# Output parts 1 to 3 of both feed-forwards by seven block products, with weight sums by adding transfers and a recorded issue order

## The chip, the cores and the metric

The kernel runs on one core of one Trainium2 chip. The metric is the device time of one execution in microseconds (us), the median of the runs that are shown. A difference of about 0.3% (3 us) is what a measurement of this kernel can tell from no change.

## What is computed

One decoder block on 512 tokens of width 1024: a feed-forward, a token-mixing layer (pooling, dilated attention and gates) and a second feed-forward, each behind an RMS norm that is shifted and scaled by a condition, then a last norm. The change is in the two feed-forwards, whose hidden width `D_FF` is 2816:

```python
def swiglu(u, w_in, w_out):
    a, b = jnp.split(u @ w_in, 2, axis=-1)
    return (jax.nn.silu(a) * b) @ w_out
...
    u = modulate(rmsnorm(h, g_norm_ffn1[l]), sh1, sc1)
    h = h + 0.5 * gt1 * swiglu(u, w_ffn1_in[l], w_ffn1_out[l])
    u = modulate(rmsnorm(h, g_norm_mix[l]), sh2, sc2)
    h = h + gt2 * token_mixing(u, cos, sin, w_in[l], w_pool[l], ...)
    u = modulate(rmsnorm(h, g_norm_ffn2[l]), sh3, sc3)
    h = h + 0.5 * gt3 * swiglu(u, w_ffn2_in[l], w_ffn2_out[l])
return rmsnorm(h, g_final)
```

The vectors shift, scale and gate come from `silu(c) @ w_ada + b_ada`, 72 columns of 128 rows.

## The kernel before

**Number format.** Activations and weights are f32. Each operand of a large product is split into a high part, rounded to fp32r (`whi`, `UH`, `HI`, `SH`), and the rest (`wlo`, `UL`, `HK`, `SL`), and a product is three matmuls: high by high, high by low, low by high (`mm3`, L364; inside `product`, L751 to L753). Everything is transposed: 128 features on the partitions, 512 tokens along the free axis.

**Weights.** A *chunk* is 128x1024 f32, 512 KB. The queue of SyncE (SP) loads it into one of a few buffers (`raw`, `X`). ScalarE (ACT) writes its high part into the ring `whi` (`split_hi`, L319) and VectorE (DVE) the rest into `wlo` (`split_lo`, L336). The rings hold seven chunks. `look(4)` puts the splits four chunks ahead of the matmuls. In the second feed-forward, the chunks of output parts 0 to 3 (`self.added`) have the rest made differently: ACT writes the negative high part into `wlo`, and GpSimd (POOL) issues a transfer that adds the raw chunk to it (L334).

**Input products.** From hidden tile 6 on in the first feed-forward (FFN1) and 4 in the second (FFN2), two hidden tiles at a time are made by `duo` (L755): seven products of quarter-size blocks instead of eight, the scheme of Strassen and Winograd. Such a group needs four chunks from memory and three sums of them; DVE makes these with four subtractions of 128x1024 (`make`, L263). A duo takes 7 x 24 matmuls of 256 columns. The sums of activations `S0` to `S2` are made once. The end of a duo adds partial results, applies silu, multiplies and splits the hidden pair into `HI` and `HK` (L776, L758, L783), one and two products later (`later`).

**Output products.** The 22 hidden tiles are taken in parts, `PARTS = ((0, 4), (4, 8), (8, 12), (12, 16), (16, 22))`. When a part's hidden tiles are there, it is multiplied by its rows of `w_out` for all eight output tiles. Parts 0 to 3 take 8 x 4 x 3 = 96 matmuls of 512 columns each (L366 to L368), and DVE adds every output tile, times the gate, to the residual `H` (L906). Parts run one duo behind: `pairs_before` gives `k1 + 2` hidden tiles made before a part's output (except part 0 of FFN2), so that the hidden tiles of a part have been split long before they are read.

**Beside it.** In FFN1, DVE also makes columns of the condition's product, one 128x1024 instruction and one 512 KB load each (`bg`, `ada_do`, L393), two beside each plain tile pair's product in part 0 and one behind each output tile of parts 1 to 3.

**Order.** The program order on each engine is the order in which the Python code calls the instructions; nothing reorders it. There are eight PSUM banks; `nb` hands six of them out in turn.

## Time and profile before

| | us |
|---|---|
| median of 3 runs | 993.51 |
| lowest and highest run | 991.79, 995.31 |
| the profiled execution, first to last instruction | 994.0 |
| FFN1, output part 0 begins (PE) | 81.2 |
| FFN1, output parts 1, 2, 3 (PE) | 141.2 to 162.9, 201.1 to 222.9, 261.1 to 282.9 |
| FFN1, last duo ends (PE) | 321.1 |
| FFN2, output parts 1, 2, 3 (PE) | 770.3 to 792.1, 830.3 to 852.1, 890.3 to 912.0 |

The profiled execution is given by its span alone; no time of the same execution measured from outside is listed, so its span stands for it, 0.5 us above the median. In the profile, PE is TensorE, and a line such as L751 is a line of the kernel. Durations of neighbouring instructions on an engine overlap by a little, so what an instruction costs its engine is the distance to the next start. "Idle before" names what ended the wait. The DMA share is the mean busy share of 16 DMA engines.

### The profile page before, as it was taken

How to read it: one execution, taken by the hardware profiler on the slowest of the kernel's cores; microseconds unless marked ns; L12 is line 12 of the kernel's file. 1: busy time of each engine (PE TensorE's matmuls, PEld its weight loads, DVE VectorE, ACT ScalarE, POOL GpSimd, SP SyncE). 2: the span in 40 equal slices, each digit the busy share in tenths (PEclk: the TensorE clock that was granted, in tenths of full speed). 3: DMA queues.
4: the chain of work that ended last, by engine and by line, in shares of the span. 5: the costliest groups of instructions: out<-in, count | busy, mean ns of one | idle time of the engine just before them, and what ended most of it. 6: DMA issues, size and time to landing. Idle time of an engine off the chain costs nothing.

```text
span 994.0 us, 16420 instructions
## 1 busy us (share of the span) xinstructions
PE 983.2 (99%) x6688; PEld 894.6 (90%) x6688; DVE 765.0 (77%) x1072; ACT 490.7 (49%) x730; POOL 45.6 (5%) x49
## 2 busy tenths in 40 slices
PE   9999999999999999999999999999999999999997
PEld 7888999989999899788879998998899898998997
DVE  7989979889797677897988877865695775647753
ACT  5453643625434553455555552555366255363553
POOL 0000000000000000007100000001001001010002
PEclk9999999999999999999999999999999999999999
DMA  9856456464564416664233336416454538264312
GB/s 347 275 196 224 149 149 198 146 196 163 188 189 119 126 56 230 201 200 144 76 106 107 106 121 211 135 44 141 128 177 115 142 118 220 86 151 128 114 33 85
DMA packets 47469, 150.14 MB, mean 151 GB/s; under 512 B 6561, under 2 KB 9377, under 8 KB 47394
## 3 DMA queue, kind: packets, MB, share of 16 engines
q1 hardware_dynamic: 44224, 140.18, 43.3%
q0 software_dynamic: 2592, 8.39, 4.6%
q8 instruction: 52, 0.85, 0.3%
q10 hardware_dynamic: 578, 0.53, 0.2%
q14 instruction: 23, 0.19, 0.1%
HBM read 135.29 MB, written 2.24 MB: 138 GB/s over the span
## 4 chain that ended last, share of the span: by engine, by line
PE 89%; DVE 3%; issue 3%; DMA 3%; SPq 1%; ACT 1%; POOL 0%; POOLq 0%; DVEq 0%; ACTq 0%
PE bank L366 14%; PE bank L368 14%; PE bank L367 14%; PE bank L751 13%; PE bank L753 12%; PE bank L752 12%; PE bank L1727 2%; PE bank L1729 1%; PE bank L1731 1%; DMA wlo<-raw 1%; SPq L1059 1%; PE bank L1403 1%; PE bank L1105 1%; PE bank L1156 1%; PE bank L1404 1%
## 5 line engine op out<-in xcount | busy, mean ns | idle before, releaser
L336 DVE TENSOR_TENSOR wlo<-raw,whi 128x1024 fp32r<-128x1024 f32 (+4 forms) x148 | 155.6, 1064 | 53.9 <-ACT whi L319 53.6
L319 ACT ACTIVATE whi<-raw 128x1024 fp32r<-128x1024 f32 (+4 forms) x162 | 146.4, 921 | 63.1 <-DVE raw L263 51.4
L751 PE MATMUL bank<-UH,whi 128*128 128x256 f32 x640 | 177.1, 277 | 0.0
L752 PE MATMUL bank<-UL,whi 128*128 128x256 f32 x640 | 177.1, 277 | 0.0
L753 PE MATMUL bank<-UH,wlo 128*128 128x256 f32 x640 | 177.1, 277 | 0.0
L366 PE MATMUL bank<-HI,whi 128*128 128x512 f32 (+1 forms) x406 | 146.2, 360 | 0.0
L368 PE MATMUL bank<-HI,wlo 128*128 128x512 f32 (+1 forms) x406 | 145.9, 359 | 0.3 <-DMA wlo<-raw 0.3
L367 PE MATMUL bank<-HK,whi 128*128 128x512 f32 (+1 forms) x406 | 145.9, 359 | 0.0
L336 DVE TENSOR_TENSOR wlo<-X,whi 128x1024 fp32r<-128x1024 f32 (+3 forms) x100 | 106.8, 1077 | 22.8 <-ACT whi L319 22.3
L753 PEld LDWEIGHTS bank<-UH,wlo 128*128 128x128 f32 x640 | 120.5, 188 | 0.0
L751 PEld LDWEIGHTS bank<-UH,whi 128*128 128x128 f32 x640 | 120.1, 188 | 0.4
L752 PEld LDWEIGHTS bank<-UL,whi 128*128 128x128 f32 x640 | 120.2, 188 | 0.0
L319 ACT ACTIVATE whi<-X 128x1024 fp32r<-128x1024 f32 (+3 forms) x104 | 96.2, 944 | 45.9 <-DVE X L263 44.5
L751 PE MATMUL bank<-SH,whi 128*128 128x256 f32 x408 | 113.1, 277 | 0.1
L752 PE MATMUL bank<-SL,whi 128*128 128x256 f32 x408 | 112.9, 277 | 0.0
L753 PE MATMUL bank<-SH,wlo 128*128 128x256 f32 x408 | 112.9, 277 | 0.0
L366 PE MATMUL bank<-UH,whi 128*128 128x512 f32 (+1 forms) x304 | 105.6, 347 | 0.0
L367 PE MATMUL bank<-UL,whi 128*128 128x512 f32 (+1 forms) x304 | 104.2, 343 | 0.1
L368 PE MATMUL bank<-UH,wlo 128*128 128x512 f32 (+1 forms) x304 | 104.0, 342 | 0.0
L368 PEld LDWEIGHTS bank<-HI,wlo 128*128 128x128 f32 x406 | 76.2, 188 | 12.4 <-DMA wlo<-raw 0.7
L366 PEld LDWEIGHTS bank<-HI,whi 128*128 128x128 f32 x406 | 76.2, 188 | 11.4
L367 PEld LDWEIGHTS bank<-HK,whi 128*128 128x128 f32 x406 | 76.3, 188 | 11.3
(349 smaller groups left out, 1870.2 us busy)
## 6 DMA issues: line engine op xcount, KB each, us to landing
raw<-wmix SPq DMA_DIRECT2D x44, 512.0 KB, 3.7
raw<-wf1i SPq DMA_DIRECT2D x31, 512.0 KB, 5.0
raw<-wf2i SPq DMA_DIRECT2D x30, 512.0 KB, 4.4
ada<-wada SPq DMA_DIRECT2D x23, 512.0 KB, 5.2
AR<-wada SPq DMA_DIRECT2D x19, 512.0 KB, 4.3
X<-wf2i SPq DMA_DIRECT2D x14, 512.0 KB, 4.5
cs<-wada SPq DMA_DIRECT2D x12, 512.0 KB, 3.6
X<-wf1i SPq DMA_DIRECT2D x12, 512.0 KB, 4.4
```

The costliest lines, as they stand in the source:

```text
L319: self.nc.scalar.activation(self.hi[:, y], r[:, x], AF.Copy)
L336: self.nc.vector.tensor_tensor(self.lo[:, y], r[:, x], self.hi[:, y], op=OP.subtract)
L366: M(ps, hi, uh, start=start, stop=False)
L367: M(ps, hi, ul, start=False, stop=False)
L368: M(ps, lo, uh, start=False, stop=stop)
L751: M(o, hi, uh, start=start and p == 0 and k == 0, stop=False, skip_group_check=True)
L752: M(o, hi, ul, start=False, stop=False, skip_group_check=True)
L753: M(o, lo, uh, start=False, stop=k == 3, skip_group_check=True)
L1059: nc.sync.dma_start(w[32 * o:32 * o + 32], t[32 * i:32 * i + 32])
L1105: nc.tensor.matmul(S[:, o], q[:, toks], k[:, ks], start=True, stop=True, skip_group_check=True)
L1156: self.nc.tensor.matmul(self.bO[64 * h:64 * h + 64, P * hp:P * hp + P], x, pt[:, (2 * h + j) * P:(2 * h + j + 1) * P], start=j == first, s ...
L1727: M(b, hi, self.UH[k], start=k == 0, stop=False)
```

## The change

Three things are changed together.

**Block products for the output.** Output parts 1, 2 and 3 of both feed-forwards (`BLOCKED`) are made from four hidden tiles by the same seven-product scheme: `out_block` takes 7 x 24 matmuls of 256 columns instead of 96 of 512. It needs, of the four hidden tiles, seven blocks of 128x256 per pair of tiles (`NB = 7 * HT`): three are the hidden values, four are sums (`split_s`). It needs four chunks of `w_out` and three sums of them, so seven chunks pass the splits instead of four. Partial results are copied out of PSUM by ACT, added by DVE, and brought into `H` by 8 updates of 256 columns and 4 of 512 (with `ng`, the negative gate). Part 1 follows its last duo at once: no duo is ahead of it any more. The first half of output product 0, which needs only the older pair of hidden tiles, stands before the duo's last product; the first half of product 1 behind it; then the second halves, which need the new pair.

**Weight sums by adding transfers.** For all block groups (17 duos, 6 output blocks, 3 gate pairs) the sums are additions, and two of four are now transfers that POOL issues with `accum_op=OP.add` (`sum`). The signs that this turns are absorbed elsewhere (`scale=-1.0` in the silu and the sigmoid, negations in `u_steps` and `mix_sums`). Of each output block's seven chunks three (`ADDED`) have their low part made by an adding transfer.

**A recorded order.** In the feed-forwards every instruction goes through `Recorder`. It keeps the matmuls in program order and sorts those of DVE, ACT, POOL and SP by a list schedule with a table of costs; then they are issued. Tiles are placed so that the matmuls' operands keep their offsets modulo 64 words (`ng` takes 8 of the 16 words of `pad0`; the scratch tiles `ut` move into the fixed pool).

The lines that carry it:

```diff
+BLOCKED = (1, 2, 3)
+ADDED = {0: (0, 3, 5), 2: (0, 3, 5)}
+NB = 7 * HT
 def pairs_before(n, part):
     k1 = PARTS[part][1]
-    return k1 if part + 1 == len(PARTS) or (n == 2 and part == 0) else k1 + 2
+    return k1 + 2 if n == 0 and part == 0 else k1
...
+            return n, [(D, n, r11, None), (D, n + 1, x0, (x0, r12, r11)), (D, n + 2, x1, (x1, r22, x0)), (D, n + 3, r21, None),
+                       (D, n + 3, r12, None), (D, n + 3, r22, None), (D, n + 3, x1, None)]
...
+    def sum(self, i):
+        if i in self.merges:
+            out, x = (self.source(z) for z in self.merges.pop(i))
+            self.nc.gpsimd.dma_start(out, x, accum_op=OP.add)
...
+    def split_s(self, j):
+        v = self.nc.vector
+        a11, a21, a12, a22 = (self.c[:, i * HT:(i + 1) * HT] for i in range(4))
+        s2, s3, s4, s1 = (self.cS[:, i * HT:(i + 1) * HT] for i in range(4, 8))
+        v.tensor_tensor(s1, a22, a21, op=OP.subtract)
+        v.scalar_tensor_tensor(s2, a11, -1.0, s1, op0=OP.mult, op1=OP.subtract)
+        v.tensor_tensor(s3, a11, a21, op=OP.subtract)
+        v.scalar_tensor_tensor(s4, a12, -1.0, s2, op0=OP.mult, op1=OP.subtract)
+        for i0, i1 in ((6, 7), (2, 6)):
+            hi, lo = self.block(j, i0, i1)
+            x = self.cS[:, (i0 + 1) * HT:(i1 + 1) * HT]
+            self.nc.scalar.activation(hi, x, AF.Copy)
+            v.tensor_tensor(lo, x, hi, op=OP.subtract)
...
+    def out_block(self, n, k0, last, hooks):
+        u = [blk[i] for i in (0, 6, 3, 1, 4, 5, 2)]
+        banks = [A, B, A, C, A, B, A]
...
+        def first():
+            self.held, self.free_look = self.pos, True
+            w[0] = self.take()
+            for g in range(2):
+                products(0, g, (0,), True)
+        def rest(end):
+            self.look(3)
+            w[1] = self.take()
+            for g in range(2):
+                products(1, g, (0,), True)
+            end()
+            for i in range(2):
+                for g in range(2):
+                    products(i, g, (1,), False)
+                    copy(*((C[g], A[g]), (p5[g], B[g]))[i])
+                    self.step()
...
+            for i in range(2, 7):
+                self.look(4)
+                w[i] = self.take()
+                for g in range(2):
+                    products(i, g, (0, 1), False)
...
+                    if n == 0 and (i, g) in ((3, 1), (5, 0), (6, 1)):
+                        self.bg()
...
     def duo(...):
+            if i == 6 and out:
+                self.product(bank, u, start, 0, out[0])
...
+            if n == 0 and i in (2, 5):
+                self.bg()
+        mult(0, C)
+        if self.blocked(j):
+            self.split_a(j)
+            end = lambda: (mult(1, A), self.split_s(j))
```

Where the order moves. First TensorE, where FFN1's duo of hidden tiles 6 and 7 meets output part 1. Before, another duo stood between them; the last duo's product ends and the output's plain matmuls begin:

```order
L751 MATMUL bank_93<-UH,whi 128x256
L752 MATMUL bank_93<-UL,whi 128x256
L753 MATMUL bank_93<-UH,wlo 128x256
L366 MATMUL bank_90<-HI,whi 128x512
L367 MATMUL bank_90<-HK,whi 128x512
L368 MATMUL bank_90<-HI,wlo 128x512
```

In the changed kernel the first half of output product 0 (bank_95 is its second bank, `HI` and `HK` the older hidden pair) is followed by the duo's last product (bank_91):

```order
L318 MATMUL bank_95<-HI,whi 128x256
L318 MATMUL bank_95<-HK,whi 128x256
L318 MATMUL bank_95<-HI,wlo 128x256
L318 MATMUL bank_91<-UH,whi 128x256
L318 MATMUL bank_91<-UL,whi 128x256
L318 MATMUL bank_91<-UH,wlo 128x256
```

So the output now stands on both sides of the duo's last product, and its second halves come 12 matmuls of 256 columns behind it.

Second VectorE at the end of the same duo. Before (`hf` is the hidden pair, `u`, `p` and `sl` its partial results, `X` and `raw` weight buffers):

```order
L790 TENSOR_TENSOR hf<-u_845,p_846 128x2x256
L263 TENSOR_TENSOR raw_68<-X,raw_68 128x1024
L336 TENSOR_TENSOR wlo<-raw_66,whi 128x1024
L814 TENSOR_TENSOR hf<-bank_91,u_844 128x2x256
L336 TENSOR_TENSOR wlo<-raw_68,whi 128x1024
L776 TENSOR_TENSOR hf<-sl,hf 128x1024
L263 TENSOR_TENSOR X<-raw_66,X 128x1024
L336 TENSOR_TENSOR wlo<-X,whi 128x256
L336 TENSOR_TENSOR wlo<-X,whi 128x768
L783 TENSOR_TENSOR HK<-hf,HI 128x1024
```

In the changed kernel, from the multiplication by the bank of the fourth product (bank_93) on; bank_91 holds the duo's last product:

```order
L318 TENSOR_TENSOR hf<-hf,bank_93 128x2x256
L318 TENSOR_TENSOR X<-X 128x1024
L318 TENSOR_TENSOR hf<-hf,bank_91 128x2x256
L318 TENSOR_TENSOR HK<-hf,HI 128x512
L318 TENSOR_TENSOR hf<-hf 128x256
L318 SCALAR_TENSOR_TENSOR hf<-hf 128x256
L318 TENSOR_TENSOR hf<-hf 128x256
L318 SCALAR_TENSOR_TENSOR hf<-hf 128x256
L318 TENSOR_TENSOR HK<-hf,HI 128x256
L318 TENSOR_TENSOR wlo<-X,whi 128x1024
L318 TENSOR_TENSOR HK<-hf,HI 128x1024
```

Eight instructions now stand between the duo's last bank and the last low part of the hidden blocks, seven of them links of one chain and one a weight split.

Third POOL. Before, its first work behind the start is the mixing layer's (`tr`, `rt` and `k` are tiles of that layer):

```order
L1797 UNCONDITIONAL_BRANCH
L1222 MEMSET tr 128x16
L1229 ISA
L1229 TENSOR_TENSOR rt_4180<-tr 128x527
L1229 TENSOR_TENSOR rt_4181<-rt_4180 64x525
```

Now 34 adding transfers stand ahead of that, these first (`X` and `raw` as targets are sums of chunks, `wlo` low parts):

```order
L2161 UNCONDITIONAL_BRANCH
L318 DMA raw2_65<-raw0_63 128x1024
L318 DMA X_117<-X_117 128x1024
L318 DMA wlo_67<-raw1_64 128x1024
L318 DMA wlo_67<-X_117 128x1024
L318 DMA raw2_65<-X_117 128x1024
L318 DMA wlo_67<-X_117 128x768
```

POOL's queue goes from no transfers in FFN1 to two per duo and five per output block, three of which write `wlo`.

430 lines of the change are left out of this document (349 added, 81 removed).

## The prediction

> **What bounds the kernel now.** I read the page first, its busy times and its chain.
>
> ```profile
> span 994.0 us, 16420 instructions
> PE 983.2 (99%) x6688; PEld 894.6 (90%) x6688; DVE 765.0 (77%) x1072; ACT 490.7 (49%) x730; POOL 45.6 (5%) x49
> PE 89%; DVE 3%; issue 3%; DMA 3%; SPq 1%; ACT 1%; POOL 0%; POOLq 0%; DVEq 0%; ACTq 0%
> ```
>
> PE is on the chain for 89% of the span. Next, whether its matmuls run without gaps (the timeline), and what the other engines do meanwhile (the windows).
>
> ```profile
> 299.81 0.28 PE L752 MATMUL bank<-UL,whi 128*128 128x256 f32 x1
> ...
> 304.00 0.28 PE L753 MATMUL bank<-UH,wlo 128*128 128x256 f32 x1
> ...
> 204.79 0.39 PE L367 MATMUL bank<-HK,whi 128*128 128x512 f32 x1
> ...
> 207.28 0.39 PE L366 MATMUL bank<-HI,whi 128*128 128x512 f32 x1
> ```
>
> The first two are 38 rows, so 37 distances: 4.19 / 37 = 0.1132 us for 256 columns. The other two are 12 rows: 2.49 / 11 = 0.2264 us for 512. A column costs the same in both.
>
> ```profile
> core 0: us, PE busy (x) PEld busy (x) DVE busy (x) ACT busy (x) POOL busy (x), PEclk, DMA share, GB/s
> 103.00:163.00 60.00, 60.00 (x435) 56.24 (x434) 52.76 (x60) 28.45 (x37) 0.00 (x0) 1.00 0.51 157
> 163.00:223.00 60.00, 60.00 (x435) 56.24 (x434) 52.77 (x67) 26.71 (x34) 0.00 (x0) 1.00 0.54 175
> ...
> 830.00:890.00 60.00, 60.00 (x435) 56.24 (x435) 38.61 (x40) 30.88 (x40) 4.19 (x5) 1.00 0.50 140
> ```
>
> Each window holds two duos and one output part. PE is busy throughout at clock 1.00. The reader is to see how near the others are: in FFN1 DVE is at 88% and the DMA at 0.54, in FFN2 DVE at 64%. So matmul time removed is gained in full only while DVE and the transfers keep up, and FFN1 has little room.
>
> **What goes from PE.** A plain part is 96 x 0.2264 = 21.73 us, the blocked one 7 x 24 x 0.1132 = 19.02 us: 2.7 us less. Six parts: **16.3 us**, 8.15 in each feed-forward. That is the most that the change can bring; I find nothing else on the chain that it shortens. If the new operands' places cost speed, the nearest slower rows are these:
>
> ```profile
> 379.77 0.28 PE L1315 MATMUL bank<-whi,UH 128*128 128x256 f32 x1
> ...
> 381.93 0.28 PE L1315 MATMUL bank<-whi,UH 128*128 128x256 f32 x1
> ```
>
> 19 rows, 2.16 / 18 = 0.120 us: on 1008 matmuls 6.9 us more. The tiles keep their offsets modulo 64 words and the weights stand in the ring where the duo's stood, so I take 0 and keep 6.9 as the other end. Sign changes, gate sums and tile placement go together at 0, bounded by the 0.3% of a measurement on either side.
>
> **What DVE gets.** Costs are distances between starts:
>
> ```profile
> 200.36 0.68 DVE L814 TENSOR_TENSOR hf<-bank,u 128x512 f32<-128x512 f32 x1
> 200.96 1.21 DVE L263 TENSOR_TENSOR X<-raw,raw 128x1024 f32<-128x1024 f32 x1
> ...
> 217.36 1.22 DVE L783 TENSOR_TENSOR HK<-hf,HI 128x1024 fp32r<-128x1024 f32 x1
> 218.49 1.22 DVE L336 TENSOR_TENSOR wlo<-X,whi 128x1024 fp32r<-128x1024 f32 x1
> 219.63 0.74 DVE L906 SCALAR_TENSOR_TENSOR H<-bank,mod,H 128x512 f32<-128x512 f32 x1
> 220.29 1.22 DVE L393 SCALAR_TENSOR_TENSOR cs<-cs,cond 128x1024 f32<-128x1024 f32 x1
> ...
> L520 DVE SCALAR_TENSOR_TENSOR H<-bank,mod,H 128x256 f32<-128x256 f32 x24 | 11.6, 482 | 8.1 <-PE bank L368 8.0
> L561 DVE TENSOR_TENSOR AR<-AR,X 128x256 f32<-128x256 f32 x8 | 3.4, 424 | 2.7 <-ACT X L521 2.6
> ```
>
> So 1.14 us for 1024 wide, 0.60 for 512, 0.66 for the 512 update, and, less the same overlap of 0.08, 0.40 and 0.35 for 256; 768 lies between, 0.87. In the changed order, from the last update of FFN1's output part 1 to that of part 2, stand 30 instructions of 1024 (17 low parts of weights, 6 sums, 5 condition columns, 2 `HK`), 2 of 768, 14 of 512, 4 updates of 512, 12 three-operand and 8 other ones of 256: 34.2 + 1.7 + 8.4 + 2.6 + 4.8 + 2.8 = **54.5 us** in a stretch for which PE now needs 3 x 19.05 = 57.2: 95%. Before it was 88%: the sums that went to POOL are replaced by chunks and hidden blocks. The next stretch, with 27 of 1024, has 51.1. In FFN2 the same count without condition columns is some 48 us of 57.2, 84%: it fits.
>
> Worse is the start of FFN1. There a duo alone stands ahead of output part 1, and DVE comes late from the start-up:
>
> ```profile
> 72.50 0.69 DVE L682 TENSOR_TENSOR HK<-u,HI 128x512 fp32r<-128x512 f32 x1 [0.70 <-ACT HI L681]
> ...
> 103.93 0.75 DVE L906 SCALAR_TENSOR_TENSOR H<-bank,mod,H 128x512 f32<-128x512 f32 x1
> ...
> 102.95 0.27 PE L372 MATMUL bank<-UH,whi 128*128 128x240 f32 x1
> ```
>
> At 103.93 DVE adds an output tile of part 0 when PE has already left that part (102.95). The first of these rows, at its end 73.2, has the same place in both orders. From there to the `HK` of 1024 that output product 2 of part 1 reads, the changed order has 33 instructions of 1024, 2 of 768, 8 updates of 512 and 8 others, 12 of 256 and 13 short ones: 37.6 + 1.7 + 5.3 + 4.8 + 4.4 + 1.7 = 55.5 us, so 128.7 at the earliest. PE reaches that product at 102.95 + 0.1 + 19.0 (duo) + 5.4 (48 matmuls of the output) = 127.6. With no idle moment DVE is 1.1 us late; with as much idle as in the window from 103 (7 of 60) 8 late. I take **3 us**, near the first end, since work is always queued there.
>
> **The new wait at every output block.** The hidden pair used to be split a duo ahead. The nearest row is the last part, where it is read at once:
>
> ```profile
> 321.31 0.60 ACT L773 ACTIVATE sl<-bank 128x512 f32<-128x512 f32 x1 [3.38 <-PE bank L753]
> 323.20 1.06 ACT L758 ACTIVATE HI<-hf 128x1024 fp32r<-128x1024 f32 x1 [1.29 <-DVE hf L776]
> ```
>
> From bank to high part took 324.3 - 321.3 = 3.0 us, and a low part of 1.2 follows. In the new chain, from the end of the duo's last product: multiplication 0.69, four 256-wide links of about 0.4, `HI` 1.06, `HK` 1.2: 4.6 us. PE has 36 matmuls, 4.1 us, of its own ahead of product 2. So 0.5 to 0.7 us is missing where DVE's queue holds nothing else. Where it does (FFN1: the split of 512 ahead and a weight split of 1.14 ahead of the last `HK`, as the order shows) some 1.5. Behind the waiting `HK` queue the next weight splits, which run four products ahead. For part 1 of FFN1 the 3 us above include it. FFN1: 3 + 2 x 1.5 = **6 us**; FFN2: 3 x 0.7 = **2.1 us**. If the recorded order fills every gap this is 0; if each chain meets a full queue, 6 x 3.
>
> **What the transfers get.**
>
> ```profile
> q1 hardware_dynamic: 44224, 140.18, 43.3%
> q0 software_dynamic: 2592, 8.39, 4.6%
> DMA to landing us min/median/max: 4.5/5.6/10.0
> 695.90 7.27 DMA wlo<-raw
> ...
> 4.00:30.00 26.00, 25.19 (x133) 20.34 (x133) 22.43 (x45) 14.01 (x21) 0.00 (x0) 1.00 1.00 367
> ```
>
> q1's 140.18 MB are 267 loads of 0.524 MB; 43.3% of 994 us makes 1.61 us of all engines for each. q0 is the adding transfers: 16 times 0.524 MB in 45.7 us, **2.86 us** each. FFN1's stretch of two duos and a block has 12 weight and 7 condition loads and 9 adds: 30.6 + 25.7 = 56.3 of 57.2 us, 98%, where it was 54%. FFN2's has 12 and 9: 45.0, 79%. The splits run four products (10.9 us) ahead, so an add that lands after 6 is hidden, one of 10 just about. The fourth row, from the chain, shows that an add in a busy stretch already stopped PE once. The last, a window of the start-up, is what a full share of 1.00 moves: 367 GB/s, 0.524 MB in 1.43 us. I charge **2 us** to FFN1 for this crowding; at nothing, 0; at the add's own longest landing (10.0 against the median of 5.6) in two of three adds per block, 3 x 2 x 4.4 = 26.
>
> [...]
>
> ACT gets three more high parts, three negative ones and eight copies of 512 per block. Its 28 us of 60 become some 37 of 57: off the path, and hidden behind PE unless a chain waits for it, which is counted above.
>
> **The sum.** 994.0 - 16.3 + 6 + 2.1 + 2 = 987.8, that is FFN1 about even (8.15 gained, 8 given back) and FFN2 6 us faster. The span stands 0.5 above the median of the runs, so I predict **987.3**.
>
> **Rivals.**
>
> *All of it is hidden.* The recorded order places the chain's links first, and idle moments of DVE in FFN2 (21 of 60 us) speak for it there; the 95% in FFN1 speaks against. It gives back at most a fourth: 978 to 983.
>
> *FFN1 gives back more than it gains, FFN2 gains.* DVE at 95% with 7 idle us in 60 before, as dependences made them: if those stay, each of two stretches takes 54.5 + 7 = 61.5 instead of 57.2, 8.6 more, in place of the 3 + 2 charged to those two: 987.3 + 3.6 = 991, and up to 996 with the start's 8 us. No measurable change.
>
> *The adds saturate the transfers, and the kernel is slower.* This is one mechanism: FFN1's stretches take the transfers' time as soon as an add costs more than (57.2 - 30.6) / 9 = 2.95 us, against 2.86 measured where the share was only 0.5. At 3.6 us an add, a fourth more, the two long stretches need 63.0 (+5.8 each), and the first, of 38.2 us with 14 loads and 7 adds, 47.7 (+9.5). That is 21 us in place of the 8 charged to FFN1: 1000. For it: the count comes to 98% already. Against: condition loads and loads of the next blocks can shift into the following duos, and at the start-up's 1.43 us a load costs less than the 1.61 counted.
>
> *It does not do what it says*: block products would have to cost more per column; the two distances above exclude that, but for the 6.9 us bound, which would give 994.
>
> **How the numbers follow.** Forecast (984 to 990.5) 0.38; all hidden 0.20; FFN1 even or worse with no measurable sum (990.5 to 996.5) 0.24; saturated 0.18. 0.3% is 3.0 us, about what a measurement can tell from no change. Faster by more: 0.38 + 0.20 = 0.58; within: 0.24; slower: 0.18. The range takes in the first three and half of the last: 980 to 999, with a tenth left out above and less than that below.
>
> **What would show it.** 168 matmuls in 19.0 us per block when not waiting; in FFN2, 57.2 to 58.5 us for two duos and a block. Waits of PE for `HI` and `HK` by DVE or ACT at output products 1 and 2, longest in part 1 of FFN1. DVE above 90% and the DMA share above 0.8 between 103 and 256 us. If FFN1's share is far below 0.9, or adds land after 6 us as before, the saturation falls. I am wrong if PE waits inside duos for weights, or if the stretches of FFN2 do not shorten.

## The result, and the profile after

| | before | after |
|---|---|---|
| median of the runs shown | 993.06 us (4 runs) | 1001.44 us (4 runs) |
| lowest, highest | 991.79, 995.31 | 999.64, 1002.94 |
| ratio, with its 95% interval | | 1.0082 (1.0062 to 1.0103) |
| span of the profiled execution | 994.0 | 997.9 (a run of 999.64) |

The changed kernel is slower by 0.8%. The forecast was 987.3, range 980 to 999, slower 0.18: wrong in sign, and the time lies outside the range.

The profiled executions differ by 3.9 us only, the medians by 8.4. In later runs of the kernel before, a time stands 2.1 us above its span, and most spans are near 991.4; so the execution that the prediction read was 2.6 us longer than its like (it holds a wait of 1.9 us in FFN2's part 0). The profiled execution after is the shortest of its four, 1.8 below the median. 3.9 + 2.6 + 1.8 makes 8.3 of the 8.4.

The page of after: span, busy times, the chain of waits by engine, the queue of the adding transfers.

```profile
span 997.9 us, 17750 instructions
PE 980.0 (98%) x7120; PEld 911.8 (91%) x7120; DVE 798.1 (80%) x1194; ACT 550.9 (55%) x827; POOL 96.3 (10%) x108
PE 86%; DVE 6%; issue 2%; DMA 2%; ACT 2%; SPq 1%; POOL 0%; POOLq 0%; DVEq 0%; ACTq 0%
q0 software_dynamic: 11088, 38.80, 20.7%
```

TensorE still carries the chain, and is hardly less busy than before (983.2) though it has 16.3 us less to do. So most of what came back does not show as idle time; part of it is that its matmuls stand further apart. Around the end of output part 1 of FFN1 (start, duration, engine, line, operation):

```profile
149.23 0.28 PE L318 MATMUL bank<-HK,whi 128*128 128x256 f32 x1
149.34 0.28 PE L318 MATMUL bank<-HI,wlo 128*128 128x256 f32 x1
149.46 0.39 PE L318 MATMUL bank<-UH,whi 128*128 128x240 f32 x2
149.69 0.28 PE L318 MATMUL bank<-UL,whi 128*128 128x256 f32 x1
...
152.51 0.28 PE L318 MATMUL bank<-SL,whi 128*128 128x256 f32 x1
```

The block's matmuls stand 0.113 us apart (0.11 and 0.12 in the rounded rows), as forecast. Then comes the matmul of 240 columns that `settle` (L570) issues ahead of the first duo of each part, in both kernels. From 149.69 to 152.51 are 24 distances: 2.82 / 24 = **0.1175 us**, where the same duo took 0.1132 before. It stays so for the 14 products of two duos and into the next block, up to a gap of 0.22 us there (192.10 to 192.32), behind which they stand at 113 again (7 distances in 0.79 us from 192.68 on). In FFN2 the same matmul once does the reverse; the block ahead had run at 0.1175 us:

```profile
835.98 0.28 PE L318 MATMUL bank<-HI,whi 128*128 128x256 f32 x1
...
836.57 0.28 PE L318 MATMUL bank<-HI,wlo 128*128 128x256 f32 x1
836.69 0.40 PE L318 MATMUL bank<-UH,whi 128*128 128x240 f32 x2
836.92 0.28 PE L318 MATMUL bank<-UL,whi 128*128 128x256 f32 x1
...
839.65 0.28 PE L318 MATMUL bank<-SL,whi 128*128 128x256 f32 x1
```

5 distances in 0.59 us ahead, 0.118; behind, 24 in 2.73: 0.1137. Behind all six blocks the 240 columns change the spacing, five times to the long one and once back.

I sorted all distances between starts of successive 256-column matmuls in both feed-forwards (100 to 380 and 665 to 1000 us) into 113 ns, 118 ns (115.5 to 125) and longer. After, 2322 of 4406 are at 118, before 485 of 3390. What they take beyond 113.2 each is 10.7 us after and 2.3 before: **8.4 us more**. Waits, and slow matmuls right behind them, are 15.2 us after and 3.7 before: 11.5 more. With the 16.3 saved: -16.3 + 8.4 + 11.5 = +3.6, against the 3.9 of the spans.

The longest wait stands in the first duo of FFN1. First TensorE's row, then ACT's rows of the same stretch:

```profile
111.98 0.58 PE L318 MATMUL bank<-SH,whi 128*128 128x256 f32 x1 [3.35 <-ACT bank L318]
112.35 0.41 PE L318 MATMUL bank<-SL,whi 128*128 128x256 f32 x1
```

```profile
107.54 1.06 ACT L318 ACTIVATE whi<-X 128x1024 fp32r<-128x1024 f32 x1 [1.97 <-DMA X<-wf1i]
108.51 1.04 ACT L318 ACTIVATE whi<-raw 128x1024 fp32r<-128x1024 f32 x1
109.45 1.04 ACT L318 ACTIVATE wlo<-raw 128x1024 fp32r<-128x1024 f32 x1
110.40 1.04 ACT L318 ACTIVATE whi<-raw 128x1024 fp32r<-128x1024 f32 x1
111.35 0.57 ACT L318 ACTIVATE bank<-bank 128x512 f32<-128x512 f32 x1
```

The third product needs its bank copied out (111.35). The sorted order has put four splits ahead of that copy, and the first of them waits for a chunk. Behind the wait the matmuls are 0.21 us apart for 13 rows, at a granted clock of 0.50 (112 to 114 us). All the waits over the whole span that come to more than 1.2 us:

```profile
PE bank L318 <- ACT bank L318: 3.4, 1, 3.4
PE bank L318 <- DVE H L318: 2.4, 3, 1.2
PE bank L318 <- DVE HK L318: 2.2, 6, 0.7
```

The `HK` line is the chain from the duo's last product to the split of the hidden pair. The `H` line is something else. Its three waits stand in product 3 of a block; this is the longest, first TensorE's row, then DVE's:

```profile
766.46 0.39 PE L318 MATMUL bank<-HI,wlo 128*128 128x256 f32 x1 [1.20 <-DVE H L318]
765.93 0.48 DVE L318 SCALAR_TENSOR_TENSOR H<-bank,mod,H 128x256 f32<-128x256 f32 x1
```

Product 3 writes one bank in two halves, and `update` adds each half to `H`. The code calls `update` behind the whole product (`later`). The recorded order puts three of these updates of a first half ahead of the last matmuls into the second half of the same bank, and TensorE then waits for DVE to get to them: 1.2 us here, where DVE's queue is full ahead of the update, and 0.6 us in the other two. The load of the stretches:

```profile
core 0: us, PE busy (x) PEld busy (x) DVE busy (x) ACT busy (x) POOL busy (x), PEclk, DMA share, GB/s
103.00:149.50 46.50, 41.49 (x339) 40.16 (x338) 41.30 (x63) 28.96 (x40) 6.97 (x8) 0.96 0.95 257
149.50:210.00 60.50, 59.65 (x509) 59.20 (x508) 55.23 (x77) 38.71 (x54) 8.66 (x10) 1.00 0.87 227
210.00:263.00 53.00, 52.72 (x450) 52.52 (x449) 47.09 (x65) 36.06 (x52) 8.67 (x10) 1.00 0.81 212
```

DVE at 89 to 91% (forecast above 90) and the DMA at 0.81 to 0.95 (above 0.8) are as forecast. From 149.5 on, TensorE is busy all the same.

Of one kernel below, e15, the profiled execution ran at a granted clock of 0.85 (0.997 in e16) and took a span of 1083.5 us, so its stages are left out.

### The profile page after: what moved, and what is told of

Its sections match the earlier page's. It is cut to its first block, busy times and chain, and to the rows that moved or that the text cites. A ratio compares the mean times of both kernels' runs of the same rounds, so it can differ in the third digit from the quotient of the medians.

```text
span 997.9 us, 17750 instructions
## 1 busy us (share of the span) xinstructions
PE 980.0 (98%) x7120; PEld 911.8 (91%) x7120; DVE 798.1 (80%) x1194; ACT 550.9 (55%) x827; POOL 96.3 (10%) x108
## 3 DMA queue, kind: packets, MB, share of 16 engines
q0 software_dynamic: 11088, 38.80, 20.7%
## 4 chain that ended last, share of the span: by engine, by line
PE 86%; DVE 6%; issue 2%; DMA 2%; ACT 2%; SPq 1%; POOL 0%; POOLq 0%; DVEq 0%; ACTq 0%
PE bank L318 52%; PE bank L566 6%; PE bank L568 6%; PE bank L567 6%; PE bank L1011 2%; PE bank L1012 2%; PE bank L1013 2%; PE bank L2091 2%; PE bank L2093 1%; PE bank L2095 1%; DVE wlo L318 1%; DVE hf L318 1%; PE bank L1766 1%; PE bank L1468 1%; DMA X<-wf1i 1%
## 5 line engine op out<-in xcount | busy, mean ns | idle before, releaser
L318 PE MATMUL bank<-UH,whi 128*128 128x256 f32 (+2 forms) x680 | 195.8, 290 | 0.0
L318 PE MATMUL bank<-UL,whi 128*128 128x256 f32 (+1 forms) x672 | 194.9, 290 | 0.1
L318 PE MATMUL bank<-UH,wlo 128*128 128x256 f32 (+1 forms) x672 | 194.7, 290 | 0.0
L318 PE MATMUL bank<-HK,whi 128*128 128x256 f32 (+1 forms) x472 | 142.4, 302 | 3.5 <-DVE HK L318 2.2
L318 PE MATMUL bank<-HI,wlo 128*128 128x256 f32 (+1 forms) x472 | 141.0, 299 | 1.3 <-DVE H L318 1.2
L318 PE MATMUL bank<-HI,whi 128*128 128x256 f32 (+2 forms) x473 | 141.1, 299 | 0.0
L318 ACT ACTIVATE whi<-raw 128x1024 fp32r<-128x1024 f32 (+3 forms) x94 | 80.8, 880 | 28.1 <-PE bank L318 15.4
L318 DVE TENSOR_TENSOR wlo<-raw,whi 128x1024 fp32r<-128x1024 f32 (+3 forms) x79 | 77.0, 994 | 8.0 <-ACT whi L318 8.0
L318 PEld LDWEIGHTS bank<-SH,whi 128*128 128x128 f32 x408 | 78.5, 192 | 3.5 <-ACT bank L318 3.5
L318 PEld LDWEIGHTS bank<-SL,whi 128*128 128x128 f32 x408 | 77.3, 189 | 0.0
```

What stands on the lines that cost most here:

```text
L318: getattr(self.real[eng], method)(*a, **k)
```

## The experiments

A stage is read from TensorE's rows: FFN1 from the first matmul of output part 0 to the first of the last part; "between" from there to the first matmul of FFN2 that reads `SH`; FFN2 from there to the first of its last part. Behind that each takes 37.2 us and the last store. Ratios are against the kernel before, run on the same chips; stages are of one profiled execution each. e4, e8, e11 and e13 stand in the text.

| kernel | median us | ratio (95%) | FFN1 | between | FFN2 |
|---|---|---|---|---|---|
| before | | | 239.9 | 392.3 | 236.9 |
| after | 1001.44 | 1.0082 (1.0062 to 1.0103) | 247.7 | 390.8 | 234.7 |
| e1 no 240 behind blocks | 994.30 | 1.0005 (0.9990 to 1.0020) | 242.4 | 390.8 | 230.3 |
| e2 256 in place of 240 | 991.84 | 0.9982 (0.9970 to 0.9994) | 240.8 | 390.9 | 232.4 |
| e3 before, no 240 at all | 1003.56 | 1.0104 (1.0091 to 1.0117) | 245.4 | 392.1 | 241.1 |
| e5 a 512 ahead of the 240 | 995.88 | 1.0016 (1.0002 to 1.0029) | 243.7 | 391.1 | 231.2 |
| e6 e2, bank copies first | 993.23 | 1.0009 (0.9998 to 1.0020) | 242.0 | 392.0 | 232.5 |
| e7 e2, no condition columns | 995.69 | 1.0026 (1.0010 to 1.0041) | 243.8 | 390.9 | 232.5 |
| e9 e2, FFN1 part 1 plain | 992.23 | 0.9987 (0.9976 to 0.9998) | 244.2 | 390.6 | 232.1 |
| e10 e2, FFN1 plain | 994.53 | 1.0019 (1.0005 to 1.0032) | 244.3 | 390.3 | 232.2 |
| e12 e2, product 3 ahead | 992.33 | 0.9995 (0.9980 to 1.0011) | 243.1 | 390.0 | 229.2 |
| e14 e10, FFN1 in program order, sums by DVE | 993.98 | 1.0005 (0.9994 to 1.0016) | 242.5 | 390.7 | 234.8 |
| e18 e14 with adding transfers | 996.25 | 1.0029 (1.0010 to 1.0049) | 244.1 | 390.7 | 234.8 |
| e15 FFN1 as before, FFN2 as e12 | 990.04 | 0.9959 (0.9944 to 0.9973) | | | |
| e16 e15, FFN1 parts 2, 3 in blocks | 989.21 | 0.9954 (0.9935 to 0.9972) | 240.9 | 390.2 | 228.7 |
| e17 e16, a bank freed sooner | 990.10 | 0.9965 (0.9953 to 0.9978) | 241.3 | 390.2 | 231.6 |

### The second spacing (e1, e2, e3, e5)

e1 leaves the 240 columns out behind blocks; the recorder still counts it, so that nothing else moves:

```diff
-            extra = 1
+            extra = 2 if part - 1 in BLOCKED else 1
...
+            k.pop("ghost", 0) or getattr(self.real[eng], method)(*a, **k)
```

> The changed kernel without the one matmul of 240 columns that stands ahead of the first duo behind each output part made of blocks (six of them; those behind plain parts stay; the recorded order of the other engines is unchanged). Theory A: this matmul shifts a phase of the matmul stream, and with it the duos go from a spacing of 113 ns to 118 ns. Then the duos that begin at 149.5, 209.9, 776 and 895 us run at 113, the extra of the slow spacing falls from about 5.6 us in FFN1 and 4.7 in FFN2 to under 1 and under 2, and the time is 991 to 995. Rival B: the 118 ns come from the places of the new operands or of the weights in the rings; then the spacing stays and the time is within 1.5 us of the changed kernel's (1000 to 1003). Rival C: they come from the load on memory by the other engines and transfers; the same numbers as B.

e2 keeps the matmul and its place and changes only its width:

```diff
-        self.nc.tensor.matmul(bank[:, :HT - SHIFT], hi, uh[:, SHIFT:HT], ...)
+        self.nc.tensor.matmul(bank[:, :HT], hi, uh[:, :HT], ...)
```

> The changed kernel with the same six matmuls kept, but 256 columns wide, like their neighbours, in place of 240 (they only fill a bank that the next matmul starts anew). If it is the odd width that shifts the phase (theory A), the result is that of the kernel without them: duos at 113 ns, 991 to 995.5 us. If any further matmul between output and duo, or the change of bank there, does it, the 118 ns stay and the time is 1000 to 1003.

e3 takes the 240 out of the kernel before (`extra = 0`).

> The kernel before without the matmul of 240 columns ahead of the first duo of each part (all of them). There the duos follow matmuls of 512 columns. Theory A: without the shift they run at the other spacing, 118 ns: 17 duos x 168 matmuls x 4.8 ns = 13.7 us more, 1004 to 1008 us; fewer if the phase differs from part to part. Rivals B and C: nothing changes but 8 matmuls of 0.1 us less: 992 to 994.

The duo behind part 1 in e2, then the first duo of e3:

```profile
147.64 0.39 PE L318 MATMUL bank<-UH,whi 128*128 128x256 f32 x2
147.87 0.28 PE L318 MATMUL bank<-UL,whi 128*128 128x256 f32 x1
...
150.59 0.28 PE L318 MATMUL bank<-SL,whi 128*128 128x256 f32 x1
```

```profile
102.59 0.28 PE L751 MATMUL bank<-UH,whi 128*128 128x256 f32 x1
102.71 0.28 PE L752 MATMUL bank<-UL,whi 128*128 128x256 f32 x1
...
105.53 0.28 PE L752 MATMUL bank<-SL,whi 128*128 128x256 f32 x1
```

In e2, 24 distances take 2.72 us, so 0.1133: theory A. In e3 they take 2.82: the kernel before turns slow in the same manner when the 240 is missing, by 1.0%, 10 us; 13.7 was the estimate for all duos, of which those of one stretch in FFN2 were at 118 already, so its 1003.56 is just under theory A's 1004 to 1008. Places of operands (B) and load (C) are out: e2 has the same operands, order and load as after, and is 9.6 us below it. The gain came as forecast (991.84 in 991 to 995.5). e1's median, 994.3, is in its range too, but its runs reach from 989.6 to 998.5.

e5 puts one matmul of 512 columns ahead of the 240, as in the kernel before:

```diff
+            pre = k.pop("pre", None)
+            if pre:
+                self.nc.tensor.matmul(*pre, start=True, stop=True, skip_group_check=True)
```

> The changed kernel with its six matmuls of 240 columns kept and one matmul of 512 columns put ahead of each (it only fills a bank that the next matmul starts anew; cost 6 x 0.23 = 1.4 us). In the kernel before, 512 columns stood ahead of the 240, and the duos ran at 113 ns all eight times. Theory A1: a matmul of 512 columns brings the stream into one phase, whatever came before, and the 240 then shift it into the good one; then all duos run at 113 and the time is 990 to 994, less spread than without the 240. Rival A2: a single one carries the phase through; then the 240 shift it from good to bad as in the changed kernel: duos at 118 in most parts, 999 to 1003.

The duos behind all six blocks ran at 113 (A1), but the time, 995.88, lies between the two ranges; it is no better than e1's and spreads as far: 991.57 to 999.05. In the profiled executions of the later kernels with this pair (e16, e17) 9 of 10 places were at 113, three of them behind a block at 118, like this one of e16 (11 distances in 1.30 us ahead, 24 in 2.74 behind):

```profile
263.01 0.28 PE L322 MATMUL bank<-HI,whi 128*128 128x256 f32 x1
...
264.31 0.28 PE L322 MATMUL bank<-HI,wlo 128*128 128x256 f32 x1
264.43 0.40 PE L321 MATMUL bank<-UH,whi 128*128 128x512 f32 x1
264.67 0.39 PE L322 MATMUL bank<-UH,whi 128*128 128x240 f32 x2
264.90 0.28 PE L322 MATMUL bank<-UL,whi 128*128 128x256 f32 x1
...
267.64 0.28 PE L322 MATMUL bank<-SL,whi 128*128 128x256 f32 x1
```

The tenth stayed at 118. So with the wide matmul ahead of the 240 the duos stood at 113 in 15 of 16 places, those of e5 among them.

### The waits at the blocks (e7, e11, e12)

e7 tests whether full queues make them. It leaves out 24 condition columns of DVE and their loads:

```diff
+            if not 24 <= j < 48:
                 self.nc.sync.dma_start(t[:, c], self.a["wada"][j * P:(j + 1) * P, c])
```

> The kernel with the six matmuls of 256 columns, without the 24 condition columns that DVE makes in FFN1 behind output part 0, nor their loads (the condition of the mixing layer is left out, its columns hold the bias alone); all other instructions stay in their order. The prediction put DVE of FFN1 at 95% and the DMA at 98%, both mostly by these, and charged 1.5 us a block to full queues and 3 to DVE's lateness at part 1. If that holds, the waits in the three blocks of FFN1 (3.6, 1.8 and 0.7 us beside the one at 108 us) fall by more than half, and the time by 3 to 5 us. If the waits are the length of the chain itself (bank, multiplication, sums, high part, low part), they change by less than 0.4 us each and the time by less than 1.5. The wait at 108 us shortens in either case, if its load comes sooner.

The waits for `HK` between 149 and 322 us are the same line in after and in e7:

```profile
PE bank L318 <- DVE HK L318: 1.1, 3, 0.7
```

Nothing changed, so it is not the load of these columns; what the prediction counted at 95% and 98% does not bind there. The time rose all the same, by 3.9 us over e2: the wait at 108 us, which was to shorten, was 3.2 instead of 2.5 and had slow matmuls behind it (2.3 more in all; the granted clock between 110 and 115 us was 0.71, in e2 1.00), and the duos after part 1 stood at 118 ns (1.7). e11 then put more matmuls ahead of the chain's end:

```diff
-                seq = seq[:6] + [(1, 0), (0, 6), (1, 1)] + [(1, i) for i in range(2, 7)]
+                seq = seq[:6] + [(1, 0), (0, 6), (1, 1)] + [(1, i) for i in (3, 2, 4, 5, 6)]
...
+            for i in (0, 3, 1, 2, 4, 5, 6):
```

> The kernel with the six matmuls of 256 columns and one output product moved in each block: product 3, which reads the hidden values themselves, stands between the second halves of products 0 and 1 instead of behind product 2. So 24 more matmuls (2.7 us) stand ahead of the first matmul that reads a sum of the new hidden pair. Leaving out DVE's condition columns left the waits at products 1 and 2 as they were (0.4 and 1.0 us), so they are the chain's length; then 2.7 us cover them: about 1.4 us in each of five blocks, 0.5 in the other, less what the new sorting does elsewhere: 985.5 to 988. If the sorting only makes the chain later, since it is wanted later, or the added order brings other waits: 990.5 to 994.

It failed: 1022.88 us (1.0306, 1.0286 to 1.0326). TensorE's rows in product 3 of the second block, then POOL's issue of a transfer with its time to landing, and a row of DVE:

```profile
196.94 0.39 PE L318 MATMUL bank<-HI,wlo 128*128 128x256 f32 x1 [2.71 <-DMA wlo<-X]
202.04 0.58 PE L318 MATMUL bank<-HI,wlo 128*128 128x256 f32 x1 [4.12 <-DVE H L318]
```

```profile
192.73 0.86 POOL L318 DMA_DIRECT2D wlo<-raw  x1 [4.61 <-ACT whi L318]
wlo<-raw POOLq DMA_DIRECT2D x1, 384.0 KB, 6.1
201.51 0.48 DVE L318 SCALAR_TENSOR_TENSOR H<-bank,mod,H 128x256 f32<-128x256 f32 x1
```

The first wait is for `wlo`: this chunk's low part is one of the three that an adding transfer makes, and product 3 now comes 2.7 us sooner. The second is not, though the next expectation says so. The transfer issued at 192.73 us landed 6.1 us later, at 198.8, and TensorE starts at 202.04, 0.05 us behind the end of an update of `H`, ahead of which DVE had weight splits and condition columns without a gap. It is the wait of half a bank again. e11's order has seven such updates, and its waits for `H` are seven, 15.6 us in all; those for transfers are two, 4.1 us. e12 gives the low part back to DVE:

```diff
-ADDED = {0: (0, 3, 5), 2: (0, 3, 5)}
+ADDED = {0: (0, 5), 2: (0, 5)}
```

> The kernel of the run before (product 3 moved ahead of the second halves of product 1) with one thing more: the low part of product 3's chunk is made by DVE again, no longer by an adding transfer. In that run TensorE waited 3 to 5 us in product 3 for exactly this low part, whose transfer was issued at 192.7 us and had landed at 202. Without it the cover of 2.7 us can show: if the chain's length is the whole wait at products 1 and 2, FFN1 (output part 0 to the last duo) takes 236 to 238 us where the kernel without the move took 240.8, FFN2 228 to 230 where it took 232.4, and the time is 984 to 988. If the new sorting brings waits elsewhere: 990 or more.

All the waits of TensorE in e12 that exceed 1.2 us in sum, to be read beside the three lines of after:

```profile
PE bank L318 <- ACT bank L318: 3.2, 1, 3.2
PE bank L318 <- DVE wlo L318: 2.3, 3, 1.5
```

The lines for `HK` and `H` are gone. `HK` is gone in e11 too: with 2.7 us more of cover the chain is hidden, so that wait was its length. `H` is gone because the order, sorted anew, has no update of half a bank ahead of its matmuls. In FFN2, waits and what follows them fell from 4.4 us (e2) to 1.0, and FFN2 to 229.2 as forecast. FFN1 did not follow (243.1): there the wait at 108 us came again (3.2 us), the three waits for `wlo` are new, and 118 ns stood in one stretch of each feed-forward. The time missed its range (984 to 988) and lies in its rival's, new waits by the new order.

### The start of FFN1 (e6, e9, e10, e14, e18)

e6 moves the two bank copies at 111 us ahead of the four splits (`block` are those splits with what depends on them):

```diff
+        return order[:a] + [i for i in x if i not in moved] + [i for i in x if i in moved] + order[b + 1:]
```

> The kernel with the six matmuls of 256 columns in place of 240, and one piece of ACT's order changed: at the first duo of FFN1 the first two copies out of the banks stand ahead of the four splits that were ahead of them (the splits that depend on these move with them; nothing else). Theory D: the wait of 2.8 to 3.6 us at 108 us is ACT waiting for a chunk with the copies behind it in its queue. Then it falls under 0.7 us, no matmuls at 213 ns follow, and of 2.7 to 4.7 us at least 2.5 are gained: 987 to 989.5 where the other took 991.8. Rival E (the prediction's step that DVE comes late from the start-up): PE only reaches the low parts of the hidden tiles sooner, and waits for DVE at output products 1 and 2 of part 1 by as much longer: 990.5 to 993.

TensorE's waits between 100 and 149 us in e6:

```profile
PE bank L339 <- DVE HK L339: 1.8, 2, 1.1
PE bank L339 <- DVE wlo L339: 1.7, 1, 1.7
```

The wait for the copy is gone, and a low part of weights and `HK` take its place: between 103 and 149.5 us waits take 6.2 us, as in e2 (6.3). That is rival E, its time (993.23) just above that range; the copy was only the first of what came late. e9 takes the block of part 1 away; e10 has `0: ()`, so all three of FFN1:

```diff
-BLOCKED = (1, 2, 3)
+BLOCKED = {0: (2, 3), 2: (1, 2, 3)}
```

> The kernel with the six matmuls of 256 columns, with output part 1 of FFN1 in plain matmuls again, behind one further duo, as in the kernel before (parts 2 and 3 of FFN1 and all three of FFN2 in blocks; sums by adding transfers and the sorted order stay). It gives up 2.7 us of matmul. The waits of TensorE between 103 and 149.5 us were 6.2 to 8.3 us in the runs so far, 2.8 to 3.6 of it (and up to 1.3 at half rate behind it) in the duo at 108 us, ahead of any block. If all of them come from the block that follows at once: 988 to 989.5. If the wait in the duo stays, which the sums and the order there make: 990.5 to 992.5.

> The same with all output parts of FFN1 plain, one duo behind, as in the kernel before; FFN2 keeps its three blocks; the weight sums by adding transfers and the sorted order stay in both. By the prediction FFN2 alone gains 8.15 - 2.1 = 6 us; by the traces so far 8.15, less 4.4 us of waits and up to 1.5 of 118-ns spacing, plus 2.9 of waits that the kernel before has there: 5 to 6.6. So 987 to 988.5, if the transfers and the sorting cost nothing in FFN1; 990 to 992, if the wait in its first duo and its half rate come from them and stay.

The block is not the main cause: with a plain part 1, 4.4 and 4.3 of e2's 6.3 us of waits stay in that stretch, though more of it in a later product (119 to 121 us), and FFN1 takes 244 us. e9 (992.23) is in its second range, e10 (994.53) above both of its own. e14 takes the transfers and the sorting away too, e18 brings the transfers alone back:

```diff
+            if i in self.dvs:
+                self.nc.vector.tensor_tensor(out, out, x, op=OP.add)
...
+        for i in order if self.sort else range(N):
```

> FFN1 in the manner of the kernel before (plain output parts one duo behind, all sums by DVE, program order), FFN2 and the mixing layer as in the changed kernel, with the 256-column matmul in place of the 240 behind blocks. FFN1 should take 239.9 us again (244.3 with adding transfers and sorting), FFN2 230 to 232.5 where the kernel before took 236.9, the stretch between 390.5 where it took 392.3: 994.0 - 1.8 - 4.4 to 6.9, so 985.5 to 988 us, the best so far. If it is not below 990, FFN1's loss comes from neither the transfers nor the sorting.

> FFN1 with plain parts and in program order, as in the run where it took 242.5 us and TensorE lost nothing between 103 and 123 us, but with two sums of weights a duo by adding transfers instead of DVE. With transfers, sorted order and plain parts that stretch lost 3.5 us and FFN1 took 244.3. If the transfers' 6 to 9 us from issue to landing make the loss: 3 to 5 us between 103 and 149.5, FFN1 245 to 248, 996 to 999 us. If the sorting made it: as with DVE, 242 to 243.5 and 993 to 995.

In e14 nothing waits before 133 us, and between 103 and 149.5 us 0.9 us are lost. TensorE's wait in that stretch in e18, then ACT's rows:

```profile
PE bank L319 <- ACT bank L319: 1.4, 1, 1.4
```

```profile
108.31 1.06 ACT L319 ACTIVATE whi<-raw 128x1024 fp32r<-128x1024 f32 x1 [4.61 <-DMA raw<-raw]
109.28 0.58 ACT L319 ACTIVATE bank<-bank 128x512 f32<-128x512 f32 x1
```

In e18 the wait for the bank copy is back, in the same duo: ACT stands 4.61 us for an adding transfer (`raw<-raw`), with the copy behind it in its queue. After TensorE's wait the matmuls stand at 118 ns up to output part 1 (43 of them between 110 and 115 us, in e14 46): 1.7 + 1.3 = 3.0 us. So the transfers bring this loss, in one execution of each kernel; the medians (993.98 and 996.25) go the same way. e18's time is in the transfers' range, its FFN1 (244.1) 0.9 short of it. With the sorted order too, the stretch loses 4.3 (e10).

e14's own time missed. FFN1 took 242.5 and not 239.9, by waits at the output parts; that they come from the condition columns, which stood elsewhere than before, is not shown. FFN2 met 118 ns again (2.9 us) and 6.1 us of waits where e2 had 4.4. By the letter of its expectation, not below 990, neither transfers nor sorting would make FFN1's loss. For the stretch to 149.5 us the rows above show otherwise; for the rest of FFN1 it stays open.

### The sorted order (e4, e8, e13)

Three kernels that leave TensorE's order alone. e4 changes one number in the recorder's model, e8 issues in program order, e13 has DVE make the two sums of the first duo.

```diff
-                fin = server + (5000. if op_add[i] else 2500.)
+                fin = server + 5000.
...
-        for i in order:
+        for i in range(N):
```

> The changed kernel with one number of the recorder's model changed: a load lands 5.0 us behind its share of the transfers instead of 2.5 (the adding transfers have 5.0 already). It sorts DVE, ACT, POOL and SP anew; TensorE's order stays. Theory D: the longest wait, 3.6 us at 108 us, where a bank copy on ACT stands in its queue behind a high part whose chunk has not landed, comes from the model's optimism: then it falls under 1.5 us, the thirteen matmuls at 213 ns behind it go too, and the time is 995 to 999 (the 118 ns stay, less or more with the phase that each wait leaves). Rival: ACT and DVE are late from the start-up whatever the order; then the wait moves to another matmul before 130 us and the time is 999 to 1003.

> The kernel with the six matmuls of 256 columns, its instructions recorded as before but issued in program order, unsorted. The run with one other number in the recorder's model cost 36 us, so the order decides much. Theory: without the list the chain's links queue behind the splits and updates that the code has ahead of them: waits of 3 to 6 us at each of six blocks, 1005 to 1030. Rival: program order is as good as the list (as it was in the kernel before): 988 to 996.

> The kernel with the six matmuls of 256 columns, and the two sums of weights of the first duo of FFN1 alone made by DVE, as before, in place of adding transfers. With all of FFN1 plain, TensorE still lost 4.3 us between 103 and 149.5 us, in the same duo. If the adding transfers (6 to 9 us from issue to landing there) with ACT's splits behind them in its queue make that loss, it falls from 6.3 to under 3.5 us and the time is 987.5 to 990. If DVE's lateness from the start-up makes it, 2.3 us of DVE more at this place lengthen it: 992 to 995.

e4 took 1036.57 us (1.0428, 1.0410 to 1.0445), e8 1023.59 (one run), e13 1007.85 (1.0140, 1.0113 to 1.0167). The largest line of TensorE's waits in each:

```profile
PE bank L318 <- DVE H L318: 16.0, 8, 3.8
```

```profile
PE bank L318 <- ACT hf L318: 10.3, 5, 2.7
```

```profile
PE bank L318 <- DVE H L318: 8.9, 7, 3.7
```

e4 and e13 missed their ranges on the far side. The list is worth some 30 us over program order (e8, against e2), and a model with later landings, as seen at 108 us, gave an order that is worse by 35 than after's. What goes wrong in e4 and e13 is above all the wait of half a bank: their orders have eight and seven updates of `H` ahead of the last matmuls into the same bank (after and e2 three, e8 and e12 none), and as many waits for `H` stand in the traces, the longest 3.8 us. The granted clock was 0.94 between 760 and 820 us of e4, and 0.991 over the whole of e4 and of e13 (0.997 in after). An experiment that re-sorts tests its edit and a new order at once; e1, e2, e5, e6 and e7 were made so that the order stays.

### A version below both (e15, e16, e17)

e15 gives FFN1 its form and order of before (as e14, with the condition columns where they stood) and FFN2 the blocks of e12 with e5's pair of matmuls behind them:

```diff
+BLOCKED = {0: (), 2: (1, 2, 3)}
+ADDED = {0: (0, 5), 2: (0, 5)}
...
+        self.nc.sort = self.n == 2
```

> FFN1 in the manner of the kernel before (plain parts, sums by DVE, program order, and now its condition columns at their old places behind the output tiles, whose move cost the last such run 2.7 us of waits there); FFN2 in blocks with product 3 ahead and its low part by DVE; behind each block one matmul of 512 columns and then the 240, which in the run with these had left every duo at 113 ns. FFN1 239.9 us, the stretch between 390.5, FFN2 229.2 less 2.3 of 118-ns spacing plus 0.7: 983 to 985.5 us with little spread. If 118 ns come back in FFN2 or FFN1 keeps waits: 987 to 990.

e16 lets parts 2 and 3 of FFN1 be blocks too, with the sorted order from there on:

```diff
+BLOCKED = {0: (2, 3), 2: (1, 2, 3)}
...
+        self.nc.sort = self.n == 2 or self.late
```

> The same with output parts 2 and 3 of FFN1 in blocks too (product 3 ahead), with adding transfers and sorted order only from behind part 1 on, when DVE has caught up with the start-up. If FFN1's loss lies at its start alone, two parts gain 2 x 2.7 us there: FFN1 235 to 236, 978.5 to 981. If the sorting or the transfers make new waits where they begin: 983 to 990.

e17 moves, in the duos of parts 0 and 1 of FFN1, DVE's multiplication with bank `A` forward, so that the bank comes free sooner:

```diff
+        if n == 0 and not self.late:
+            mult(1, A)
+            mult = lambda *x: None
```

> The kernel of the run before with one instruction earlier: in the part of FFN1 that is issued in program order, the second multiplication of a duo, which reads its last bank, stands directly behind the first instead of behind two output tiles and two condition columns. There TensorE stood 2.0 us at 148.8 us for that bank and then ran at half rate, 3.8 us in all. If that bank is the whole wait: 984.5 to 986, FFN1 237 us. If the hidden pair's or the weights' low parts are next: 987 to 989.

All three are below both kernels, by 0.35 to 0.46%, and their intervals overlap. e15 (990.04) is at the edge of its second range, e16 (989.21) in its rival's, e17 (990.10) above both of its own. In e16, FFN2 is 8.2 us below before, but FFN1 1 us above: TensorE stood 1.8 us for a bank in part 1, and then ran at half rate (seven matmuls of 512 columns 0.43 us apart). e17 freed that bank, the wait went, and behind it, where the sorted order begins, stood these, between 100 and 210 us:

```profile
PE bank L322 <- ACT u L322: 1.5, 1, 1.5
PE bank L322 <- ACT HI L322: 1.2, 1, 1.2
```

The tenth place at 118 ns is also e17's, in FFN2 (231.6 for 228.7).

## Why the prediction was wrong

- **The step that failed** stands in "What goes from PE": "The tiles keep their offsets modulo 64 words and the weights stand in the ring where the duo's stood, so I take 0 and keep 6.9 as the other end." The block products mostly run at 113 ns (what they take beyond it is 1.4 us over all six), so the 19.02 us per block nearly hold. But their neighbours do not: the 240 columns that the diff leaves in place, with which the duos behind matmuls of 512 ran at 113 ns (before; in e3, without them, at 118), were followed by 118 ns behind five of the six blocks of 256. That is 7.3 of the 8.4 us, on duos, on instructions that the change did not touch; shown by e1 and e2, and from the other side by e3. The bound of 6.9 was for the wrong 1008 matmuls, and it entered only a rival ("It does not do what it says", 994). The trace of before held the sign: from 722.5 to 770.3 us 406 distances in a row are 118 ns. The prediction read the spacing of duos at 300 us alone.
- **The other terms come near in sum.** Forecast: -16.3 + 6 + 2.1 + 2 = -6.2, span 987.8. With the 8.4 and the waits as measured (11.5 for 10.1) it is 997.6, against 997.9. Without most of the second spacing the stages come near the forecast: FFN1 "about even" (+2.5 in e1, +0.9 in e2), FFN2 "6 us faster" (-6.6, -4.5). The medians of e1 and e2, though, are 7.0 and 4.5 us above 987.3: the executions that were profiled are the second shortest of 12 and the fourth of 10. So even without this step's error the gain is 0.2% (e2), where 0.6% was forecast.
- **The wait at every block** is, for `HK`, the chain's length, as counted (e11, e12: with 2.7 us more of cover it is gone): in e2, 2.4 us for parts 2 and 3 of FFN1 (3 forecast) and 1.9 for the three of FFN2 (2.1 forecast). That the condition columns lengthen it in FFN1 is refuted by e7, which leaves the weight split ahead of the last `HK` in its place. Another 2.3 us in FFN2 are waits for `H`, a cost of the recorded order that the prediction had at nothing: it expected of that order only that it may fill gaps.
- **The start of FFN1** cost more (8.2 us in the first stretch after, 3 forecast), and begins sooner: in the duo ahead of part 1, where ACT's splits wait and hold a bank copy. The adding transfers bring this (e18), without any block. DVE's lateness, the forecast's reason, shows behind it (e6). The prediction had costed the transfers' landing only against the splits four products ahead, not against what ACT has queued behind a split.
- **Crowding and saturation.** An add cost 20.7% of 997.9 over 74 adds = 2.79 us (2.86 before), not 3.6; the DMA share was 0.81 to 0.95. The saturation rival had the right sign and nearly the right time (1000) by a cause that did not occur: e7 took the condition loads away, 7 of the 28 transfers of a stretch, and the waits at the blocks stayed.
- **What was announced as a sign of error** came: the stretches of FFN2 did not shorten (the 240 columns behind one block stand at 776.2, behind the next at 836.7: 60.5 us; before, two duos and a part took 60.0).
- A small slip in a sum (127.6 for 127.5 us) changes nothing.
- Open: what the two spacings are, what a wait does to them, and where the longer executions of one kernel lose their time; only one execution of each is profiled.

## What to carry to other kernels

When a stream of matmuls is tuned to a spacing, find out which instruction sets it up and on what it depends, and read the spacing of the neighbours of a change, not of the new matmuls alone: 4% on instructions that no diff touches ate the gain here. A wait for a chain is judged by its length against the work ahead, and a kernel that takes load away shows at once whether queues have a part in it. Where a list schedule makes the order, hold the order fixed in an experiment, or the lottery of a new one (16 and 35 us here) hides the edit. Much of that lottery was one pattern: the list let an update read half of a bank ahead of the last matmuls into the other half, and the stream of matmuls then waited for whatever stood ahead of the update in DVE's queue.

## What the runs showed of the hardware

- Spacing, read as distances between the starts in TensorE's rows of the profiles: in the feed-forwards, matmuls of 256 columns in fp32r stood 113 or 118 ns apart, and kept to it where nothing disturbed them (after, from 149.69 us on: 14 products, 40 us at 118); those of 512 columns stood 226 ns apart (before, 204.79 to 207.28 us). One matmul of 240 columns between those of 256 was followed by the other spacing, both ways (six of six places in after); one of 256 was not (six of six in e2). Behind gaps and waits all of it occurred in after: 118 became 113 behind the gap of 0.22 us at 192.32 us, 113 became 118 behind the wait of 0.58 us at 826.46, and 113 stayed behind the one of 0.70 us at 196.58.
- Half rate behind waits: in after, behind the wait of 3.35 us, 13 matmuls of 256 columns stood 0.213 us apart, and the granted clock was 0.50 between 112 and 114 us (0.96 between 103 and 149.5 us). In e11, behind 4.12 us, 7 distances were 0.214 us. In e10, behind 2.2 us, 13 distances were 0.213 us (granted clock 0.96 between 103 and 149.5 us), and in e16, behind 1.8 us, seven of 512 columns were 0.43 us. But in e2, behind 2.5 us, the next matmuls stood at 113 ns (granted clock 1.00 between 110 and 115 us), and in e4, behind 3.39 us at 207.55 us, 10 distances from 207.77 us on took 1.14 us. So in these traces the length of the wait alone did not tell whether half rate followed.
